# A hardware loop in place of 62 separate reduce instructions on VectorE

## The chip, the cores and the metric

The kernel runs on one core of one Trainium2 chip. The metric is the device time of one execution in microseconds (us), and lower is better. "Before" is the kernel as it was; "after" is the changed one. VectorE is called DVE in the profile, ScalarE ACT, GpSimd POOL and SyncE SP; a "q" after the name (DVEq, SPq) is that engine's instruction sequencer.

## The reference

```python
# x: 64 x 256 x 8192 float32
def reference(x):
    return np.mean(x, axis=2)
```

These are 16,384 rows of 8,192 numbers, 536.87 MB to be read once. Two rows on each of 128 partitions make a "pair tile" of 8 MiB. There are 63 pair tiles, and the last 256 rows are loaded in five smaller pieces.

## The kernel before

Three buffers (NBUF = 3) go round. SyncE issues a load when VectorE has finished with the buffer. VectorE waits for the load and sums both rows with one instruction.

```python
    R = 2
    NP = rows // (R * P) - 1          # 63
    NBUF = 3
    # ...
        def sync_program(eng):
            for t in range(NP):
                if t >= NBUF:
                    eng.wait_ge(dve_sem, t - NBUF + 1)
                eng.dma_start(bufs[t % NBUF][:], x_pair[t]).then_inc(in_sems[t % NBUF], 16)
            # ... the last 256 rows in five pieces, then three output DMAs
        def vector_program(eng):
            for t in range(NP - 1):
                eng.wait_ge(in_sems[t % NBUF], 16 * (t // NBUF + 1))
                eng.tensor_reduce(
                    res[:, t, :],
                    bufs[t % NBUF][:].rearrange("p (r l) -> p r l", r=R),
                    X,
                    ADD,
                ).then_inc(dve_sem, 1)
            # ... eight more instructions for the last tiles
```

The first three loads are moved ahead of the program's start-up code. TensorE and ScalarE turn the sums round and scale them at the end; ScalarE and GpSimd are idle for nearly the whole run.

## Time and profile before

| | before |
|---|---|
| time, median of 3 runs | 1247.26 us (1247.18 to 1247.38) |
| span in the profile | 1245.3 us |
| HBM read | 536.87 MB at 431 GB/s |
| VectorE busy | 87% |
| one pair reduce | 17.22 us |
| idle before a pair reduce | 2.13 us |
| issue to landing of a pair load | 40.78 us |

Four lines of the profile's page of the kernel before follow: the span; the busy share of the DMA engines and the rate of transfer in 40 equal slices of the span; and the group of the pair reduces (busy time in us, mean ns of one, idle time before them and what ended it).

```profile
span 1245.3 us, 194 instructions
...
DMA  9999999999999999999999999999999999999998
GB/s 434 421 425 438 438 438 438 436 421 423 438 438 438 438 438 436 410 434 438 438 438 438 438 432 413 436 438 438 436 438 438 421 423 438 438 438 436 438 438 341
...
L119 DVE TENSOR_REDUCE res<-buf 128x2 f32<-128x16384 f32 x62 | 1067.6, 17220 | 152.9 <-DMA buf<-in_x_dram 152.9
```

The DMA engines are at 9 tenths in 39 of the 40 slices, and all of VectorE's idle time before the reduces was ended by a load. The stream is the limit. A few lines of the chain of waits (start us, duration us, what) show one round of a buffer:

```profile
215.66 17.23 DVE res L119
...
232.91 40.78 DMA buf<-in_x_dram
...
273.71 17.23 DVE res L119
```

A load takes 40.78 us from issue to landing, although pair tiles begin only 19.35 us apart. More than half of the 40.78 us is waiting behind the two loads ahead of it. So the reduces in this chain do not set the pace, although they are part of it.

The timeline (start us, duration us, engine, line, operation, and in brackets the idle time before it) of the kernel before has one place that I did not ask about when I predicted:

```profile
854.24 17.22 DVE L119 TENSOR_REDUCE res<-buf 128x2 f32<-128x16384 f32 x1 [2.13 <-DMA buf<-in_x_dram]
873.59 17.22 DVE L119 TENSOR_REDUCE res<-buf 128x2 f32<-128x16384 f32 x1 [2.13 <-DMA buf<-in_x_dram]
893.70 17.22 DVE L119 TENSOR_REDUCE res<-buf 128x2 f32<-128x16384 f32 x1 [2.88 <-DMA buf<-in_x_dram]
```

The step from 873.59 to 893.70 is 20.11 us, where nearly all others are 19.35, and the idle time is 2.88 instead of 2.13 us. The DMA queues of the same kernel, for the stretch from 1 to 1244 us (queue, kind, packets, MB, share), show a guest there:

```profile
q1 hardware_dynamic: 9866, 536.94, 99.9%
q14 instruction: 1, 0.01, 0.0%
```

One packet in this stretch, of 8,192 bytes, is not the kernel's data: the profile gives its kind as "instruction", and I call it an instruction fetch.

### The profile page before, as it was taken

Reading aid. Unit: us, or ns where it says so; the run is one execution under the profiler, and the core shown is the slowest. Engines: PE = TensorE matmul, PEld = TensorE weight load, DVE = VectorE, ACT = ScalarE, POOL = GpSimd, SP = SyncE. Lnnn points to the kernel's source line nnn. Section 1 sums busy time; section 2 is a strip of 40 time slices with the busy share of each in tenths; the row PEclk is TensorE's granted clock in tenths of the full one; section 3 lists DMA queues with packets and bytes.
Section 4 is the critical chain, followed back from the end, with each engine's and each line's share of the span. In section 5 each row is a group of like instructions: output and inputs, shape, how many; then the busy total and the mean of one; then the engine's idle time right before and its main releaser. Section 6 shows DMA issues by size and latency. Waiting matters only on the chain.

```text
span 1245.3 us, 194 instructions
## 1 busy us (share of the span) xinstructions
PE 1.7 (0%) x6; PEld 0.6 (0%) x6; DVE 1085.6 (87%) x70; ACT 17.2 (1%) x14; POOL 0.8 (0%) x7
## 2 busy tenths in 40 slices
PE   0000000000000000000000000000000000000000
PEld 0000000000000000000000000000000000000000
DVE  2898988988889889898898988989889898898897
ACT  0000000000000000000000000000000000000005
POOL 0000000000000000000000000000000000000000
DMA  9999999999999999999999999999999999999998
GB/s 434 421 425 438 438 438 438 436 421 423 438 438 438 438 438 436 410 434 438 438 438 438 438 432 413 436 438 438 436 438 438 421 423 438 438 438 436 438 438 341
DMA packets 9876, 536.95 MB, mean 431 GB/s; under 512 B 1107, under 2 KB 1171, under 8 KB 1427
## 3 DMA queue, kind: packets, MB, share of 16 engines
q1 hardware_dynamic: 9874, 536.94, 99.7%
q14 instruction: 2, 0.01, 0.0%
HBM read 536.87 MB, written 0.07 MB: 431 GB/s over the span
## 4 chain that ended last, share of the span: by engine, by line
DMA 70%; DVE 29%; SPq 0%; issue 0%
DMA buf<-in_x_dram 70%; DVE res L119 29%; SPq L101 0%; DVE part L137 0%; SPq L95 0%; DVE fint L145 0%; DVE fint L147 0%; DVE fin L143 0%
## 5 line engine op out<-in xcount | busy, mean ns | idle before, releaser
L119 DVE TENSOR_REDUCE res<-buf 128x2 f32<-128x16384 f32 x62 | 1067.6, 17220 | 152.9 <-DMA buf<-in_x_dram 152.9
L153 ACT ACTIVATE buf<-buf 128x1024 f32<-128x1024 f32 (+3 forms) x5 | 15.0, 2994 | 1222.3 <-DMA buf<-in_x_dram 1222.2
L127 DVE TENSOR_REDUCE res<-buf 128x1 f32<-128x8192 f32 x1 | 8.7, 8686 | 2.1 <-DMA buf<-in_x_dram 2.1
L129 DVE TENSOR_REDUCE res<-buf 128x1 f32<-128x4096 f32 x1 | 4.4, 4420 | 1.0 <-DMA buf<-in_x_dram 1.0
L131 DVE TENSOR_REDUCE part<-buf 128x1 f32<-128x2176 f32 x1 | 2.4, 2419 | 1.1 <-DMA buf<-in_x_dram 1.1
L178 PE MATMUL ps<-ident,res 128*63 128x128 f32 x2 | 0.7, 430 | 1231.5 <-DVE res L127 1231.5
L153 ACT ACT_TABLE_LOAD x1 | 1.3, 1283 | 1.8 <-PEq L214 1.8
L133 DVE TENSOR_REDUCE part<-buf 128x1 f32<-128x1024 f32 x1 | 1.2, 1219 | 0.1
L137 DVE TENSOR_REDUCE part<-buf 128x1 f32<-128x512 f32 x1 | 0.7, 687 | 0.7 <-DMA buf<-in_x_dram 0.7
L153 ACT ACTIVATION_READ_ACCUMULATOR buf<-buf 128x1 f32 x5 | 0.9, 186 | 0.0
L178 PEld LDWEIGHTS ps<-ident,res 128*63 128x63 f32 x2 | 0.3, 205 | 1231.4 <-issue 1231.4
L182 PE MATMUL psone<-ident,res 128*1 128x128 f32 x2 | 0.6, 421 | 0.0
L181 PE MATMUL psone<-ident,res 128*1 128x128 f32 x2 | 0.6, 397 | 4.7 <-DVE res L129 4.7
L163 ACT ACTIVATE outsb<-ps 63x128 f32<-63x128 f32 x2 | 0.4, 264 | 0.0
L79 POOL TENSOR_SCALAR_AFFINE_SELECT ident<-ident 128x128 f32<-128x128 f32 x1 | 0.3, 292 | 0.2 <-POOL ident L77 0.2
L165 ACT ACTIVATE out1sb<-psone 1x128 f32<-1x128 f32 x1 | 0.3, 267 | 1.5 <-PE psone L182 1.5
L182 PEld LDWEIGHTS psone<-ident,res 128*1 128x1 f32 x2 | 0.3, 128 | 0.2
L145 DVE STREAM_TRANSPOSE fint<-fin 128x32 f32<-128x32 f32 x1 | 0.2, 212 | 0.0
L147 DVE TENSOR_SCALAR fint<-fint 128x32 f32<-128x32 f32 x1 | 0.2, 181 | 0.0
L77 POOL MEMSET ident<- 128x128 f32 x1 | 0.2, 204 | 0.0
L143 DVE TENSOR_REDUCE fin<-part 128x1 f32<-128x6 f32 x1 | 0.2, 158 | 0.0
L76 POOL MEMSET fin<- 128x32 f32 x1 | 0.1, 125 | 1.3 <-POOLq L214 1.3
(5 smaller groups left out, 0.5 us busy)
## 6 DMA issues: line engine op xcount, KB each, us to landing
buf<-in_x_dram SPq DMA_DIRECT2D x1, 4096.0 KB, 31.1
buf<-in_x_dram SPq DMA_DIRECT2D x1, 2304.0 KB, 17.3
buf<-in_x_dram SPq DMA_DIRECT2D x1, 1024.0 KB, 19.4
buf<-in_x_dram SPq DMA_DIRECT2D x63, 40.8
buf<-in_x_dram SPq DMA_DIRECT2D x1, 512.0 KB, 20.2
buf<-in_x_dram SPq DMA_DIRECT2D x1, 256.0 KB, 20.3
out_dram<-outsb SPq DMA_DIRECT2D x1, 63.0 KB
out_dram<-out1sb SPq DMA_DIRECT2D x1, 0.5 KB
```

What stands on the lines that cost most here:

```text
L79: eng.affine_select(out=ident[:], in_=ident[:], compare_op=mybir.AluOpType.not_equal, fill=1.0, base=0, pattern=[[-1, P]], channel_multipl ...
L119: eng.tensor_reduce(res[:, t, :], bufs[t % NBUF][:].rearrange("p (r l) -> p r l", r=R), X, ADD,).then_inc(dve_sem, 1)
L127: eng.tensor_reduce(res[:, t, 0:1], bufs[t % NBUF][:, :L], X, ADD).then_inc(dve_sem, 1)
L129: eng.tensor_reduce(res1[:, 0:1], buf1[:, : L // 2], X, ADD).then_inc(dve_sem, 1)
L131: eng.tensor_reduce(part[:, 0:1], buf2[:, :s0], X, ADD).then_inc(dve_sem, 1)
L133: eng.tensor_reduce(part[:, 1:2], buf2[:, offs[1] : offs[1] + s1], X, ADD).then_inc(dve_sem, 1)
L137: eng.tensor_reduce(part[:, 2:3], buf2[:, offs[3] : offs[3] + CH[3]], X, ADD).then_inc(dve_sem, 1)
L153: eng.activation(src, src, Copy, accum_out=dst).then_inc(act_sem, 1)
L163: eng.activation(outsb[:, :, r], ps[r][:], Copy, scale=inv).then_inc(cp_sem, 1)
L178: eng.transpose(ps[r][:], res[:, :, r], ident[:]).then_inc(pe_sem, 1)
L181: eng.matmul(psone[:], res1[:, 0:1], ident[:], start=True, stop=False)
L182: eng.matmul(psone[:], res1[:, 1:2], ident[:], start=False, stop=True).then_inc(pe_sem, 1)
```

## The change

The intent is a shorter VectorE program: one loop body of three reduces, one for each buffer, run 20 times. The value to wait for and the output's address are now computed in registers. Two pair tiles stay outside the loop.

```diff
         def vector_program(eng):
-            for t in range(NP - 1):
-                eng.wait_ge(in_sems[t % NBUF], 16 * (t // NBUF + 1))
+            def pair(k, trip, dst):
+                eng.wait_ge(in_sems[k], trip)
                 eng.tensor_reduce(
-                    res[:, t, :],
-                    bufs[t % NBUF][:].rearrange("p (r l) -> p r l", r=R),
-                    X,
-                    ADD,
+                    dst, bufs[k][:].rearrange("p (r l) -> p r l", r=R), X, ADD
                 ).then_inc(dve_sem, 1)
+
+            trips = (NP - 1) // NBUF
+            with eng.Fori(0, trips) as i:
+                for k in range(NBUF):
+                    pair(k, 16 * i + 16, res[:, bass.ds(NBUF * i + k, 1), :])
+            for t in range(trips * NBUF, NP - 1):
+                pair(t % NBUF, 16 * (t // NBUF + 1), res[:, t, :])
```

## The prediction

> **What bounds the kernel now.** The input stream. The page's DMA row is at 9 tenths in 39 of 40 slices; 536.87 MB are read at 431 GB/s. In the timeline pair tiles start on VectorE every 19.35 us (41.27, 60.62, 79.98): one 8 MiB load at about 433 GB/s. A pair's reduce takes 17.22 us, and before each VectorE sits idle 2.13 us; the waits put all 152.9 us of this down to the load. So VectorE is 87% busy but is not the limit.

> The chain of waits alternates load (70%) and reduce (29%), which looks as if the reduce mattered: load 40.78 + reduce 17.23 + 0.04 = 58.05 us = 3 x 19.35, the round of one buffer. But of the 40.78 us from issue to landing only about 19.35 is the load's own transfer. The first load, with nothing ahead of it, was reduced 21.5 us after its issue. The other 19.3 us are queueing: at an issue, about 2 us of one load and the whole next one are still ahead. A later reduce shortens the queueing, not the stream.

> **What the change removes, adds, moves.** Same reduces, loads and bytes. 62 straight-line instructions with constant waits become 20 trips of three and 2 peeled tiles. Added per trip: a register add and a compare-and-branch; per tile: register arithmetic for the wait's value and the output's address, and a wait against a register, perhaps resolved by the sequencer before it hands the reduce over. [...] much can be done while the previous reduce runs.

> **How much is on the critical path.** None. VectorE has 2.13 us of slack a tile, 6.4 a trip; below that the landings keep the pace, and the queue holds another 19 us before the DMA engines run dry. The end (chunked last tiles) is outside the loop and begins with landings that don't move. The loop's set-up has the first load's 21 us to hide in.

> **Predicted:** 1247.3 us, 8 times in 10 within 1246.7 to 1248.3. Faster by over 2%: 0.5%; within 2%: 97%; slower: 2.5%.

> **What would show each step.** Right: 62 pair reduces of 17.22 us, still 19.35 us apart, DMA row at 9, 431 GB/s; [...] the sum per buffer still 58.05; last landing near 1242.2 us, within 1 us. Wrong: another releaser than the load, gaps in the DMA row, starts over 19.4 us apart, a pair reduce over 17.3 us.

> **What would make it wrong.** A register wait, a computed address or the back edge costing over 2.13 us a tile (6.4 us a trip) without overlapping the reduce: then VectorE sets the pace and each further 0.1 us a tile costs 6 us (0.5%). [...]

The forecast's sum is the median before, 1247.26 us, with nothing added for the critical path: 1247.3 us. Measured after the change: a compare-and-branch of 50 to 56 ns, a register add of 40 ns, a waiting register instruction of 69 ns on VectorE's sequencer before each looped reduce, and 0.11 us more from landing to reduce. That much of the work can run during the reduce before is shown by b_dve and a_dve below: 60 reduces in 1027.69 us, without the loop and with it.

## More of the kernel before

By "completion" the text means one of the 16 records that a load leaves in the trace as it lands (before: 336 for the 21 loads of each buffer). They are taken as one for each of the 16 DMA engines, since the packet records of before show 16 chains of 64 KiB packets side by side.

## The result, and the profile after

| | before | after |
|---|---|---|
| time, median | 1247.22 us (1246.54 to 1247.38, 4 runs) | 1246.26 us (1245.68 to 1246.42, 4 runs) |
| span in the profile | 1245.3 us | 1244.7 us |
| idle before the 62 pair reduces | 152.9 us | 152.3 us |
| issue to landing of a pair load | 40.78 us | 40.66 us |
| last pair load landed (from the completion records) | 1222.64 us | 1222.02 us |

The ratio is 0.9993, with a 95% interval of 0.9975 to 1.001. A ratio here is the mean time of one kernel's fast runs over the mean of the other's fast runs of the same rounds, so it is not quite the ratio of the medians quoted. The median lies 0.44 us under the low end of the range. Differences here are well under one part in a thousand, and the interval includes 1, so the argument below rests on the records in the traces and not on the times alone.

The same lines of the page after:

```profile
span 1244.7 us, 315 instructions
...
DMA  9999999999999999999999999999999999999998
GB/s 436 415 430 438 438 438 438 430 413 438 438 438 438 438 436 411 434 438 438 438 438 438 425 417 438 438 438 438 438 432 411 438 438 438 438 438 436 417 428 373
...
L121 DVE TENSOR_REDUCE res<-buf 128x16384 f32 (+1 forms) x62 | 1067.6, 17220 | 152.3 <-DMA buf<-in_x_dram 152.3
```

The 62 reduces are as long as before, and loads still end all of the idle time before them. One round of a buffer in the chain of waits after:

```profile
233.13 40.66 DMA buf<-in_x_dram
...
273.82 0.07 DVEq L121
...
273.94 17.23 DVE res L121
...
291.18 40.66 DMA buf<-in_x_dram
```

There is a new piece, DVEq, of 0.07 us between landing and reduce. With its hand-over it comes to about 0.11 us, and the load's 40.78 us have become 40.66: what the loop adds on one side, the queue gives back on the other. These are the groups of the new instructions (count; ns min/median/max):

```profile
L121 DVEq FUSED_REGOPS  x60: 69/69/69, 22.0 to 1164.0; - x60
```

```profile
L126 DVEq FUSED_REGOPS  x20: 62/63/63, 1.9 to 1106.3; - x20
L126 DVEq ALU_OP  x20: 40/40/52, 60.8 to 1164.1; - x20
L126 DVEq COMPARE_BRANCH  x20: 50/56/56, 60.9 to 1164.2; - x20
```

The first, 69 ns, stands before each of the 60 looped reduces and waits for the load. The others come once a trip, just after a reduce has started (but for the first FUSED_REGOPS, at 1.9 us).

The timeline after, at the place of the long step before, has no such step:

```profile
854.48 17.22 DVE L121 TENSOR_REDUCE res<-buf 128x16384 f32 x1 [2.13 <-DMA buf<-in_x_dram]
873.82 17.22 DVE L121 TENSOR_REDUCE res<-buf 128x16384 f32 x1 [2.12 <-DMA buf<-in_x_dram]
893.17 17.22 DVE L121 TENSOR_REDUCE res<-buf 128x16384 f32 x1 [2.14 <-DMA buf<-in_x_dram]
```

In the queues from 1 to 1244 us the instruction fetch is gone. The only line is:

```profile
q1 hardware_dynamic: 9866, 536.94, 99.9%
```

That is the difference to be explained: a step of 20.11 us that became one of 19.35 us, 0.76 us, and with it one packet that is gone. (The 63rd load lands only 0.62 us earlier, as its other completions come a little later after the change, the 1st by 0.16 us.) The completion records say more than the timeline. The table has, in us, the 15th and the 16th (last) completion of the loads around that place; the 1st is given too.

| load | 1st before | 15th before | 16th before | 1st after | 15th after | 16th after |
|---|---|---|---|---|---|---|
| 45th | 873.14 | 873.49 | 873.57 | 873.26 | 873.60 | 873.68 |
| 46th | 892.50 | 892.92 | 893.67 | 892.62 | 892.96 | 893.03 |
| 63rd | 1221.46 | 1221.90 | 1222.64 | 1221.62 | 1221.93 | 1222.02 |

At the 46th load one completion of the 16 falls 0.75 us behind the 15th, and it is still 0.74 us behind at the 63rd. Fifteen engines come as they did after the change; one is late, and the load counts as landed when that one is done. In the packet records the fetch (8,192 bytes) starts at 877.72 us, just as one engine's 64 KiB data packet ends, and takes 0.32 us (the records do not number the engines; packets are matched here by where one ends and the next starts). The engine's next data packet starts at 878.03 us, 0.31 us after the one before it ended, and takes 3.08 us, where the median is 2.42. Data packet, fetch and data packet follow each other; the 0.31 us that the fetch takes between two data packets is called the turn below. The engine loses 0.31 us to the turn and 3.08 - 2.42 = 0.66 us to the slower packet after it, 0.97 us in all. The last of the 16 engines began its packet of this round at 877.95 us, where the engine that was hit would have begun at 877.72; so 0.23 us were to spare, and 0.97 - 0.23 = 0.74 us are what the load lost. VectorE waited for the last completion: its reduce of the 46th load starts at 893.70 us, 0.03 us after the 16th completion (893.67) and 0.78 us after the 15th (892.92).

### The profile page after: what moved, and what is told of

It reads as the page before. It is cut to its first block, busy times and chain, and to the rows that moved or that the text cites. A ratio compares the mean times of both kernels' runs of the same rounds, so it can differ in the third digit from the quotient of the medians.

```text
span 1244.7 us, 315 instructions
## 1 busy us (share of the span) xinstructions
PE 1.7 (0%) x6; PEld 0.6 (0%) x6; DVE 1085.6 (87%) x70; ACT 17.2 (1%) x14; POOL 0.8 (0%) x7
## 3 DMA queue, kind: packets, MB, share of 16 engines
HBM read 536.87 MB, written 0.07 MB: 431 GB/s over the span
## 4 chain that ended last, share of the span: by engine, by line
DMA 70%; DVE 29%; issue 0%; SPq 0%; DVEq 0%
DMA buf<-in_x_dram 70%; DVE res L121 29%; DVEq L121 0%; SPq L101 0%; DVE part L143 0%; SPq L95 0%; DVE fint L151 0%; DVE fint L153 0%; DVE fin L149 0%
## 5 line engine op out<-in xcount | busy, mean ns | idle before, releaser
L121 DVE TENSOR_REDUCE res<-buf 128x16384 f32 (+1 forms) x62 | 1067.6, 17220 | 152.3 <-DMA buf<-in_x_dram 152.3
## 6 DMA issues: line engine op xcount, KB each, us to landing
buf<-in_x_dram SPq DMA_DIRECT2D x1, 2304.0 KB, 17.3
buf<-in_x_dram SPq DMA_DIRECT2D x1, 1024.0 KB, 19.4
```

The source lines that it names most:

```text
L121: eng.tensor_reduce(dst, bufs[k][:].rearrange("p (r l) -> p r l", r=R), X, ADD).then_inc(dve_sem, 1)
```

## The experiments

The theory, called FETCH: the kernel before lost 0.7 to 0.8 us to one instruction fetch of VectorE's, in the way of the stream on one DMA engine, and that lag is not made up to the end (0.75 us at the 46th load, 0.74 us at the 63rd); the loop makes VectorE's program too short for the fetch, and otherwise costs nothing. Rivals: SCATTER (it is chance), SPACING or LOOP (the loop's later issue of the loads is itself what helps).

All kernels gave correct results except b_dve and a_dve, which are not in the table and have a section of their own. "Against before" is the mean of the kernel's runs less the mean of before's runs in the same rounds. A "border" is a place in an engine's program at which it stops and goes on after a pause with no other releaser in the trace (VectorE after its 61st instruction in b_pad128, GpSimd after every 128 in a_pool512), and a "block" is the 128 instructions between two such places.

| label | what it is | fetches in the stream (by) | median, us | against before, us |
|---|---|---|---|---|
| r_after | after, again | 0 | 1246.36 | -0.66 |
| a_half | half looped, half not | 0 | 1246.23 | -0.97 |
| a_unroll12 | loop of 12 tiles | 0 | 1246.33 | -0.74 |
| a_pool128 | after, GpSimd fetches | 1 (GpSimd) | 1246.58 | -0.39 |
| b_act14 | no loop, 14 tiles on ScalarE | 1 (ScalarE) | 1246.49 | -0.62 |
| a_pad64 | after, VectorE fetches | 1 (VectorE) | 1246.80 | -0.33 |
| a_straddle12 | loop across a block's border | 1 (VectorE) | 1246.93 | -0.10 |
| b_pad20 | before, fetch moved | 1 (VectorE) | 1247.02 | +0.09 |
| b_pad128 | before, a second fetch | 2 (VectorE) | 1247.89 | +0.90 |
| a_pool512 | after, GpSimd fetches | 4 (GpSimd) | 1248.51 | +1.53 |
| b_act11 | no loop, 11 tiles on ScalarE | 0, one at the end | 1247.22 | +0.21 |
| b_act9 | no loop, 9 tiles on ScalarE | 0, one at the end | 1246.80 | -0.40 |

Which engine fetched is not in the records; it is inferred from which program was made longer or shorter.

Two more readings of the traces, one profile of each kernel, are steadier than the times. First, the 63rd load landed at 1221.88 to 1222.02 us in all six kernels without a fetch in the stream, be they looped (after, r_after, a_half, a_unroll12) or not (b_act11, b_act9), and at 1222.03 to 1224.00 us in all with one or more (a_pool128 and b_act14, with the smallest sums below, at 1222.03 and 1222.10). Second, the sum of above (the turn and the slower packet, less what the engine had to spare) gives the delay: 0.72 us in b_pad20 (long step less 19.35: 0.73), 0.49 in a_straddle12 (0.46), 0.33 in b_act14 (0.33), 0.22 in a_pool128 (0.19), 0.97 for the second fetch of b_pad128 (0.95) and 2.39 for the four of a_pool512 (2.40 over two steps). a_pad64 does not fit it. The slower packet took 3.08 us with VectorE's fetches in mid-stream and 2.77 to 2.80 us with those put down to GpSimd and ScalarE, where the median is 2.42 us; the turn took 0.31 us with either.

### r_after: the changed kernel again

> The changed kernel again, unaltered. Theory FETCH: in the kernel before, one 8 KiB instruction fetch 877.7 us into the span sits on one of the 16 DMA engines, its neighbouring 64 KiB packet takes 3.08 instead of 2.42 us, and one start-to-start step of VectorE is 20.11 instead of 19.35 us, a delay that is never made up; the loop makes VectorE's program too short for that fetch. It expects 0.6 to 1.0 us less than before in the same rounds, no instruction packet between 1 and 1240 us, no step over 19.6 us. Theory SCATTER: the 1 us is chip and run scatter; it expects a difference under 0.3 us either way.

Measured: 1246.36 us (1245.99 to 1246.60) against 1247.12 us (1246.32 to 1247.21) for before; the means differ by 0.66 us. There was no instruction packet in the stream and no pair step above 19.50 us. The ratio, 0.9995 with an interval of 0.9981 to 1.0008, doesn't exclude 1, and one run of before fell among those of after. That fits FETCH in size, but by times alone SCATTER would not be out. The next runs put the fetch where I choose.

### b_pad20: does the long step move with the fetch?

```diff
         def vector_program(eng):
+            for j in range(20):
+                eng.memset(pad[:, j : j + 1], 0.0)
```

> Kernel before with 20 one-column memsets on VectorE ahead of its first wait (hidden in the first load). FETCH: the fetch is VectorE's and comes when its program has run a fixed number of instructions, so it moves 20 tiles earlier, from 877.7 to about 491 us, and the one long step of about 20.1 us moves with it; time as before within 0.3 us. SCATTER: the long step stays where it was, near 873 us, or is gone, and has nothing to do with the fetch.

Measured: 1247.02 us (1246.78 to 1247.59), as before. The fetch came at 490.7 us. This is the timeline there:

```profile
467.30 17.22 DVE L122 TENSOR_REDUCE res<-buf 128x2 f32<-128x16384 f32 x1 [2.14 <-DMA buf<-in_x_dram]
486.64 17.22 DVE L122 TENSOR_REDUCE res<-buf 128x2 f32<-128x16384 f32 x1 [2.12 <-DMA buf<-in_x_dram]
506.72 17.22 DVE L122 TENSOR_REDUCE res<-buf 128x2 f32<-128x16384 f32 x1 [2.86 <-DMA buf<-in_x_dram]
```

The long step, 20.08 us, has moved from the 45th to the 25th tile, by 20 tiles for 20 instructions. At 873 us nothing is left of it. SCATTER falls for the step: it belongs to the fetch, and the fetch comes after the same number of VectorE's instructions in both kernels (during the reduce that follows the first 44: 44 reduces in before, 20 memsets and 24 reduces here).

### b_pad128: a second fetch

The same edit with 128 in place of 20.

> Kernel before with 128 one-column memsets on VectorE ahead of its first wait, 8 KiB of instructions more. FETCH: two instruction packets in the stream instead of one (one within the first load, one near 878 us); if both sit on the same DMA engine, 0.5 to 0.8 us longer than before, if not, up to 0.8 us. SCATTER: as before within 0.3 us.

Measured: 1247.89 us (1247.73 to 1247.92), every run above every run of before in the same rounds; the means differ by 0.90 us, a little over the 0.5 to 0.8 that I expected. Fetches came at 9.3 and at 878.5 us. The timeline of VectorE at the start (count at the end of a line):

```profile
1.84 1.75 DVE L119 MEMSET pad<- 128x1 f32 x61 [1.84 <-PEq L217]
3.96 1.93 DVE L119 MEMSET pad<- 128x1 f32 x67 [0.37 <-issue]
22.75 17.22 DVE L122 TENSOR_REDUCE res<-buf 128x2 f32<-128x16384 f32 x1 [16.86 <-DMA buf<-in_x_dram]
```

### a_pool128 and a_pool512: the loop stays, an idle engine fetches

```diff
             ).then_inc(prep_sem, 1)      # the end of GpSimd's program
+            eng.wait_ge(dve_sem, 30)
+            for j in range(128):         # 512 in the second kernel
+                eng.memset(pad[:, j : j + 1], 0.0)
```

> The changed kernel with 128 one-column memsets on the otherwise idle GpSimd after the 30th tile. FETCH: an instruction packet in the stream near 585 us from GpSimd, one step about 0.7 us longer in the next two tiles, and the time 0.5 to 0.9 us longer than the changed kernel, that is equal to before within 0.3 us, though VectorE still runs the loop. A rival, SPACING (the loop helps since each load is issued 0.11 us later after its landing): equal to the changed kernel, 0.6 to 1.0 us under before.

Measured: 1246.58 us (1246.45 to 1246.67). The fetch came at 606.5 us, the next step was 19.54 us. That is a miss in size: 0.2 us of step and 0.27 us of mean time over r_after (1246.58 and 1246.31), not 0.5 to 0.9. The neighbouring data packet took 2.77 us, 0.35 more than the median and not 0.66. The spread from the 1st to the 16th completion rose at the load that follows from 0.63 to 0.83 us, by 0.2. In the packet records the engine lost 0.31 us to the turn and 0.35 us to the slower packet, but it was not the last of the 16: it would have begun its packet at 606.50 us, the last one began at 606.94, so 0.44 us were to spare and 0.22 us remain. This run is too small a dose to decide against SPACING; the next one has four.

> The changed kernel with 512 one-column memsets on GpSimd after the 30th tile, 4 blocks of 128 instructions. One block cost 0.25 us of time there, less than VectorE's 0.7, as its DMA engine was not the last of the 16 and had 0.2 us to spare. FETCH: 4 instruction packets between 600 and 630 us; if each adds 0.3 to 0.35 us to the same DMA engine, the spread of the 16 completions of a load rises by 0.9 to 1.3 us and the time to 1247.2 to 1247.8. If the packets fall on several engines: 1246.5 to 1246.7.

Measured: 1248.51 us (1248.34 to 1248.83), more than the 1247.2 to 1247.8 that I expected. Four instruction packets came at 606.4, 611.9, 617.4 and 622.9 us. The timeline there:

```profile
600.34 6.06 POOL L91 MEMSET pad<- 128x1 f32 x182 [597.79 <-DVE res L125]
602.41 17.22 DVE L125 TENSOR_REDUCE res<-buf 128x16384 f32 x1 [2.13 <-DMA buf<-in_x_dram]
608.08 4.28 POOL L91 MEMSET pad<- 128x1 f32 x128 [1.68 <-issue]
613.57 4.28 POOL L91 MEMSET pad<- 128x1 f32 x128 [1.21 <-issue]
619.05 2.50 POOL L91 MEMSET pad<- 128x1 f32 x74 [1.19 <-issue]
624.34 17.22 DVE L125 TENSOR_REDUCE res<-buf 128x16384 f32 x1 [4.71 <-DMA buf<-in_x_dram]
```

GpSimd stops at a border and then after every 128 instructions, 1.2 to 1.7 us each time. VectorE's reduce at 624.34 waited 4.71 us for its load. The 16th completion of that load is 2.58 us behind the 15th (624.20 and 621.62), and of the 63rd load still 2.39 us (1224.00 and 1221.61). So four fetches on an idle engine, with VectorE's loop untouched, cost 2.27 us (1248.55 less the 1246.28 of a_unroll12, means of the same rounds). The loads are issued with the loop's 0.11 us delay here too, and the gain is gone threefold. That shows that a fetch costs time; that the later issue gains nothing is shown not by this run but by a_half, a_straddle12 and b_act11 below. The size follows from the packet records: each of the four fetches starts as a packet of the same, ever later, engine ends, and costs it 0.31 us for the turn and 0.35 us for a packet of 2.77 us, 2.62 us in all (unrounded); 0.23 us were to spare (606.42 against 606.65), which leaves 2.39.

### a_pad64: the loop with VectorE's fetch given back

The loop of the kernel after, behind 64 memsets like those of b_pad20.

> The changed kernel with 64 one-column memsets on VectorE ahead of the loop. In the run with 128 memsets on the kernel before, VectorE paused 0.43 us after its 61st instruction and fetched 8 KiB for each 128 instructions. Theory FETCH: this kernel crosses that place once, in the first 10 us, and has one fetch there on VectorE's late DMA engine; all landings 0.6 to 0.9 us later than in the changed kernel from the first tile on, time 1247.1 plus or minus 0.2, like before, though the pair tiles run in the loop. Theory LOOP (the loop itself, with its later issues, is what gains): 1246.3, like the changed kernel.

Measured: 1246.80 us (1246.51 to 1247.24), a fetch at 9.0 us; its mean lies 0.65 us over that of a_half in the same rounds (1246.84 and 1246.19). By its times the looped kernel has lost most of its gain, though it is looped as before, which speaks against LOOP. But the median is 0.1 us under the range for FETCH, and the one profile, of its slowest run, does not show the late engine to the end: at the 2nd load the 16th completion is 0.43 us behind the 15th, at the 4th, after a shift of all engines, 0.23 us, and at the 63rd 0.23 us, no more than in a_half without a fetch (0.26). The 63rd load lands 0.88 us later than in a_half, and all of this is a shift of all engines: the 1st completion is at 1221.99, where a_half had 1221.10 and after 1221.62. So this run alone does not show how its fetch cost the time. Such shifts of all engines, 0.1 to 0.9 us in sum, are in most traces within the first 200 us, in before and after alike; I do not know their cause.

### a_half: half a loop

```diff
-            trips = (NP - 1) // NBUF
+            trips = (NP - 1) // NBUF // 2
```

> Only the first 30 tiles in the loop (10 trips), the other 32 as separate instructions with constant waits. FETCH: some 51 instructions stand in VectorE's program, short of the 61 after which it fetches; no instruction packet in the stream, time 1246.3 plus or minus 0.2 like the changed kernel. LOOP: half of the gain, 1246.7 to 1246.9. The waiting register instruction (69 ns a tile in the changed kernel) is there 30 times instead of 60; start-to-start steps 19.35 in both halves, one step of about 19.24 at the seam.

Measured: 1246.23 us (1245.98 to 1246.38), no instruction packet in the stream, the full gain with half the loop. At the seam one step is 19.23 us: the 0.11 us that the waiting register instruction costs is taken back there, once. This is what FETCH expects and LOOP does not.

### b_dve and a_dve: what the loop costs when VectorE sets the pace

```diff
-                eng.dma_start(bufs[t % NBUF][:], x_pair[t]).then_inc(in_sems[t % NBUF], 16)
+                if t < NBUF or t == NP - 1:
+                    # as before
+                else:
+                    eng.dma_start(bufs[t % NBUF][:, :L], x_pair[t][:, :L]).then_inc(in_sems[t % NBUF], 16)
```

The results are wrong: half of each tile is old data. b_dve has this edit on the kernel before, a_dve on the kernel after.

> Kernel before with the loads of tiles 3 to 61 cut to half their bytes (wrong result on purpose: the reduce takes the other half from an older tile), so that VectorE and not the stream sets the pace. Both theories of the loop's own cost expect start-to-start steps of 17.22 to 17.26 us and a time near 1105 to 1115 us; it is the base for the next run.

> The changed kernel with the same half loads: what the loop costs when VectorE sets the pace. Theory HIDDEN: with the data already there, the register instruction of the next tile and the back edge run during the reduce before, so steps and time equal the base within 0.5 us. Theory EXPOSED: 0.11 us a tile (69 ns register instruction and its 40 ns hand-over), steps of 17.35 us, 6 to 7 us longer; with an exposed back edge (62 + 40 + 56 ns a trip) 9 to 10 us.

Measured: 1111.08 us (1110.97 to 1111.17) and 1111.18 us (1110.79 to 1111.39). The timelines of VectorE, first of b_dve and then of a_dve; the line merges 60 reduces that follow each other without idle time:

```profile
60.66 1027.69 DVE L122 TENSOR_REDUCE res<-buf 128x2 f32<-128x16384 f32 x60 [2.12 <-DMA buf<-in_x_dram]
```

```profile
60.89 1027.69 DVE L124 TENSOR_REDUCE res<-buf 128x16384 f32 x60 [2.12 <-DMA buf<-in_x_dram]
```

The stretch of 60 reduces is 1027.69 us in both (17.13 us a reduce, a little under the 17.22 that I expected). HIDDEN holds: with the data there, the register work, the wait and the branch all run during the reduce before, and the loop costs nothing that can be seen. The 0.11 us a tile of the kernel after are exposed only since its waiting instruction has to wait for the load. I had overlooked a second reading of this pair: b_dve has an instruction fetch at 759.3 us and a_dve has none, and the stretches are equal all the same. With half loads, where the stream is not the limit, a fetch costs nothing that can be seen.

### a_unroll12 and a_straddle12: a loop across a block's border

```diff
-            trips = (NP - 1) // NBUF
+            U = 12
+            trips = (NP - 1) // U
             with eng.Fori(0, trips) as i:
-                for k in range(NBUF):
-                    pair(k, 16 * i + 16, res[:, bass.ds(NBUF * i + k, 1), :])
+                for k in range(U):
+                    pair(k % NBUF, 16 * (U // NBUF) * i + 16 * (k // NBUF + 1),
+                         res[:, bass.ds(U * i + k, 1), :])
```

> The changed kernel with 12 tiles a trip, 5 trips: the loop body is 30 instructions, the program 42, within the first 61. FETCH: no instruction packet in the stream, 1246.3 plus or minus 0.2; the waiting register instruction again 69 ns before 60 reduces. Base for the next run.

Measured: 1246.33 us (1246.06 to 1246.44), no instruction packet in the stream.

> The same 12-tile loop behind 36 one-column memsets, so that the place after the 61st instruction lies inside the loop body and each of the 4 back edges and each later pass crosses it. Theory KEPT [...]: one instruction packet in the stream, at about the second tile of the first trip, and the time of before, 1247.1 plus or minus 0.3. Theory REFETCH (a back edge over the border fetches the block again): 5 to 9 packets, all on the same late DMA engine at 0.7 to 0.8 us each, 1249 to 1253 us, with long steps of about 20 us at each trip.

Measured: 1246.93 us (1246.54 to 1247.20), one instruction packet in the stream, at 199.9 us. KEPT holds: the 4 back edges cross the border (the place after the 61st instruction) with this one packet and no new fetch. The packet came eight tiles later than I expected, because I had counted wrongly: in the list of VectorE's instructions 36 memsets, 1 register move and the first 24 of the loop's body make 61, and these end with the 10th tile's reduce. That reduce starts at 196.22 us and the fetch follows 3.7 us later; in the kernel before it followed 4.1 us after the start of the 45th reduce. In the one profile the step at the fetch was 19.81 us and the 16th completion went to 0.45 us behind the 15th (215.88 and 215.43); the mean of five runs is 0.65 us over a_unroll12, and 0.10 us under before. So with one fetch in the stream the loop gains next to nothing: LOOP falls here.

### b_act11, b_act14 and b_act9: no fetch in the stream, and no loop

These are straight-line kernels with constant waits, in which ScalarE takes every fifth tile (every fourth, every sixth). VectorE's program gets shorter by as many instructions.

```diff
+        ON_ACT = list(range(4, 59, 5))       # 11; 14: range(4, 60, 4); 9: range(4, 57, 6)
...
-            for t in range(NP - 1):
+            for t in (u for u in range(NP - 1) if u not in ON_ACT):
... and on ScalarE, ahead of its last tile:
+            for t in ON_ACT:
+                eng.wait_ge(in_sems[t % NBUF], 16 * (t // NBUF + 1))
+                for r in range(R):
+                    acc(res[:, t, r : r + 1], bufs[t % NBUF][:, r * L : (r + 1) * L])
... and the semaphore counts that follow from it
```

> Kernel before, no loop and no register anywhere, but 11 of the 62 pair tiles (every fifth) are reduced on the idle ScalarE, so that VectorE's program is 59 instructions long, short of the 61 after which it fetched. Theory FETCH: no instruction packet in the stream, no step of 20.1 us, time 1246.3 plus or minus 0.2, as with the loop (if ScalarE, now with some 58 instructions, fetches in its turn, up to 0.3 us more). Theory LOOP: 1247.1, as before, since nothing is looped.

Measured: 1247.22 us (1246.85 to 1247.48). By its time alone this run would have spoken for LOOP, and it is a miss. Its trace says otherwise: no instruction packet in the stream, and the 63rd load landed at 1221.96 us, as with the loop (1222.02) and not as before (1222.64), though no load is issued later for a register wait. The gain was there and was lost at the end. An 8 KiB fetch came at 1244.1 us, among the packets of the last output DMA. This is SyncE's wait for that DMA, in us, first in b_act11 and then in after (total, times, longest):

```profile
SPq L121 <- DMA out_dram<-fint: 1.9, 1, 1.9
```

```profile
SPq L114 <- DMA out_dram<-fint: 1.0, 1, 1.0
```

By the instructions' own times the wait grew from 1.00 to 1.96 us. So a fetch seems not to need a long stream to cost something: here it met the very last transfer. The packet records show part of how: the last of the four output packets starts at 1244.65 us, as the fetch ends, 0.39 us after the other three. The other 0.6 us of the wait are not explained.

> As the run with 11 tiles on ScalarE, but with 14: VectorE's program is 56 instructions, ScalarE's some 70. The run with 11 had no fetch in the stream and its last pair load landed 0.68 us earlier than before, but an 8 KiB fetch at 1244.1 us, 1.2 us after VectorE's last instruction, sat ahead of the last output packet and the final wait took 1.96 instead of 1.00 us. Theory V-END (VectorE, 59 instructions and a few closing ones, reached its 61st there): no fetch between 1240 and 1246 us here, final wait 1.0 us. Theory S-END (ScalarE reached the end of its block): ScalarE now reaches it earlier, a fetch in the stream and none at the end; time 1246.3 plus 0.2 to 0.7.

> The same with 9 tiles on ScalarE: VectorE's program is 61 instructions, ScalarE's some 54. V-END: [...] the fetch moves into the stream, between 1050 and 1230 us, or stays at the end; time 1246.9 to 1247.4. S-END: no fetch by ScalarE, none at 1244 us, and time 1246.3 plus or minus 0.2 unless VectorE fetches too.

Measured: b_act14 took 1246.49 us (1246.28 to 1246.76), with no fetch at the end, the final wait back at 1.0 us, and a fetch in the stream at 877.5 us; this is a program whose VectorE part is short and whose ScalarE part is long. Its 16th completion was then 0.33 us behind the 15th, and its time is near that of a_pool128 with its single fetch by GpSimd. b_act9 took 1246.80 us (1246.41 to 1246.91), with no fetch in the stream, one at 1243.6 us, half a microsecond earlier than in b_act11, and a final wait of 1.3 us. The fetch at the end comes earlier when VectorE's program is two instructions longer, and not at all when it is three shorter; that favours VectorE (V-END), though b_act9's mean of 1246.73 is a little under what V-END expected, and b_act14 came out as S-END expected too (a fetch in the stream, none at the end), while b_act9 did not (a fetch at the end, where S-END had none). Whose fetch it was at the end is therefore not settled. That the straight-line kernel reaches the loop's stream without any register or branch is.

No version beats the kernel after: a_half and a_unroll12 equal it.

## Why the prediction was right or wrong

- *The stream bounds the kernel; VectorE has slack.* Right. The reduces stayed at 17.22 us and 19.35 us apart, and loads ended all 152.3 us of idle time before them.
- *The register work a tile.* Measured: 0.07 us plus hand-over, 0.11 us from landing to the reduce, and nothing more on the first of a trip. The quantity that I had named to show it, VectorE's idle time before a reduce, did not rise (2.13 us in both): with landings 19.35 us apart and reduces of 17.22 us it has to stay, whatever shifts the start. I chose the wrong view. The time from issue to landing did fall, from 40.78 to 40.66 us. The two half-load kernels show that the rest of the loop's work is hidden.
- *A compare-and-branch a trip.* The trace after has 50 to 56 ns in 20 trips, off the critical path.
- *"Same reduces, loads and bytes".* This is the step that failed. The kernel's data are the same; the bytes on the DMA engines are not. With the straight-line program there was a fetch of 8 KiB in the middle of the stream, at 877.72 us. With the loop that fetch is gone. I read the totals of the page before, and the line with the instruction queue was on it, but I did not ask where in the span those packets lay.
- *"How much is on the critical path. None."* Wrong in consequence. A fetch was on it, worth 0.76 us by the step in the timeline and 0.66 to 0.97 us in the means of the loop kernels without it, about a sixteenth of one percent. The instruction fetch was in the prediction, but only as a danger of the new kernel at its back edges (after has no fetch from 1 to 1244 us with 20 trips, a_straddle12 one with 4 back edges over a border). It was the old kernel that fetched.
- *Within 1246.7 to 1248.3 us.* Missed by 0.44 us, for the reason just given. I had set the low end by the scatter of three runs, with no room for any gain. "Within 2%" was right.

## What to carry to other kernels

In this kernel, bound by its DMA stream, a single packet of 8,192 bytes, an instruction fetch, was on the critical path: the load it hit was as late as the latest of its 16 completions, 0.75 us behind the 15th. What the fetch cost was what it took from its engine less what that engine had to spare against the last one (0.97 - 0.23 us in the kernel before, 0.66 - 0.44 us in a_pool128). So in a kernel bound like this look at where in the span the packets of other queues lie, and at single long steps in an otherwise even timeline. The hardware loop on VectorE, with its 2.13 us of slack a tile, cost nothing in time here, and helped a little by keeping the program short of the fetch (0.66 to 0.97 us); what mattered was the program's length and not the loop (the 63rd load landed at 1221.96 us in b_act11, without a loop, and at 1222.02 us in after). The gain is under one part in a thousand, so a timing alone would hardly have shown it; a step that can be moved at will by 20 instructions did.
